# Seven pairs of hidden tiles start the MLP early instead of six, the last token tile's transposes stand nine steps behind its norm, and the last block's split comes first with its low part on GpSimd

## The chip, the cores and the metric

The kernel runs on one core of one Trainium2 chip. The engines are named as in the profile: PE (TensorE, matrix products; PEld its weight loads), DVE (VectorE), ACT (ScalarE), POOL (GpSimd), SP (SyncE, which here only issues DMAs). The metric is the device time of one execution in microseconds, and lower is better.

## What is computed

Two decoder layers over 1024 tokens of width 1024, in float32. Layer 0 mixes with a sparse attention of three branches, layer 1 with a sliding window; each is followed by a squared-ReLU MLP with 4096 hidden units. Cut to what the change touches:

```
for i in range(DEPTH):                       # DEPTH = 2
    ...
    y = mixer(modulate(rms_norm(x, norm_g[i, 0]), sh1, sc1))
    x = x + (1 + g1) * rms_norm(y, norm_g[i, 1])
    h = modulate(rms_norm(x, norm_g[i, 2]), sh2, sc2)
    a = relu(h @ mlp_w_up[i])                # 1024 x 1024 @ 1024 x 4096
    y = (a * a) @ mlp_w_down[i]
    x = x + (1 + g2) * rms_norm(y, norm_g[i, 3])
```

## The kernel before

**Products.** A float32 product is made of three matmuls of rounded parts (`mm3`, L572 to L574): each operand is split into a high part (`hh` of the tokens, by ACT at L1250; the first half of `wt` of the weights, by ACT at L1339) and a low part, value minus high part (`hl`, L1251, and the second half of `wt`, L1340, both DVE). A product of a 128-wide weight tile with 512 tokens over four k-tiles is 12 matmuls of 128x512.

**Seven products for eight.** `mlp_up` takes the hidden units as 16 pairs of 128-wide tiles, and the operands as 2x2 blocks. The tokens' blocks are B11 and B21 (token tiles 0 to 3, the two halves of the width) and B12 and B22 (token tiles 4 to 7). Of each pair it makes seven products with sums and differences of blocks. Products 1 (with B11) and 2 (with B21) need token tiles 0 to 3 alone; products 6, 5, 7, 3 and 4 need T1 = B12 - B11, B22 - T1, B22 - B12, B22 itself and B21 - (B22 - T1). Product 3 takes B22 as it is. Weights are summed for products 6 (L1322, L1323, DVE), 7 and 3 (L1329, L1333, POOL).

**The early products.** The MLP's products begin while the output projection of the attention is still finishing its last token tiles. `order` lists products 1 and 2 of the first `PAIRS0` pairs first (the early products, twelve for six pairs), then products 6, 5, 7, 3 and 4 of each of those pairs (the dependent products), then seven products for each later pair. An early pair's weights come as 512 KB for its products 1 and 2 (`load(q, True)`), and later again in two halves of 512 KB for the others (`load(q, False)`). `before(i)` says which weights are loaded and split ahead of the i-th product.

**The last token tile.** Token tiles arrive one by one. `done` queues for each: the stages of its norm (residual sum L522 on DVE, square on ACT, root on POOL L451, scaling into `xr` on DVE L472), then idle steps, then the steps of `tile(t)`: eight transposes on PE (`turn`, L1234), eight evacuations with the adaLN scale and shift on ACT (`put`, L1245), and `near` (L1266 on DVE for T1, L1267 on POOL for B22 - B12). For the last tile follow: `minus` on DVE (L1257, two of 128x1024: B22 - T1), the splits, and `minus` on POOL (L1257, two: B21 - (B22 - T1)). Each split is two pairs of instructions (two k-tiles each).

**Order and buffers.** The steps are handed out by `go`, `later` and `chain` between the products; from the program written so, a scheduler makes the row of instructions of each engine, and an engine takes its row strictly in order. The tiles of 4 KB per partition (`hr`, `hh`, `hl`, `wt`, `w`, `u`, `sx`) share 40 slots: an instruction or DMA that fills a tile waits until the slot's tile before it is done with. After its products a hidden pair's results (`u`) are combined on POOL (L1415, L1426) and written to DRAM by SP.

Of the kernel before, what the change touches and what calls it, by code (L numbers as in the profile page):

```python
# [9 lines left out]
F32 = mybir.dt.float32  # L10
# [4 lines left out]
ALU = mybir.AluOpType  # L15
# [7 lines left out]
NT = S // P  # L23
# [5 lines left out]
SLOTS = 40  # L29
UT = HID // P  # L30
LEAD_DOWN = 14
PAIRS0 = 6
TURN = (10, 20)
SIDE2 = 40
AHEAD = 3
DL = 4
# [57 lines left out]
class Trunk:  # L94
# [1126 lines left out]
    def up_setup(self, w_up, col):  # L1221
# [6 lines left out]
        nc = self.nc  # L1228
        R, raw, pts = {}, {}, {}

        def turn(t, xr, c):
            pts[t, c] = pt = self.bank()
            for k in range(4):
                nc.tensor.transpose(pt[:, k * P:(k + 1) * P], xr[t][:, (4 * c + k) * P:(4 * c + k + 1) * P], self.ident)  # L1234
            if c == 1:
                xr.pop(t)

        def put(t, c):
            pt, (A, B) = pts.pop((t, c)), col()
            for k in range(4):  # L1240
                n = (t // 4, c, k // 2)
                if t % 4 == 0 and k % 2 == 0:
                    raw[n] = self.slot("hr", F32, [P, 2, 512])
                f = 4 * c + k
                nc.scalar.activation(raw[n][:, k % 2, (t % 4) * P:(t % 4 + 1) * P], pt[:, k * P:(k + 1) * P], AF.Identity,  # L1245
                                     scale=A[:, f:f + 1], bias=B[:, f:f + 1])

        def split(p, r):
            hi, lo = (self.slot(x, F32R, [P, 2, 512]) for x in ("hh", "hl"))
            nc.scalar.activation(hi, r, AF.Copy)  # L1250
            nc.vector.tensor_tensor(lo, r, hi.bitcast(F32), op=ALU.subtract)  # L1251
            R.setdefault(p, []).append((hi, lo))

        def minus(eng, out, x, y):
            if out not in raw:
                raw[out] = self.slot("hr", F32, [P, 2, 512])
            eng.tensor_tensor(raw[out], raw[x], raw[y], op=ALU.subtract)  # L1257

        b11, b21, b12, b22, t1 = (lambda j, n=n: (*n, j) for n in ((0, 0), (0, 1), (1, 0), (1, 1), (2, 0)))

        def near(t, j):

            if t1(j) not in raw:
                raw[t1(j)] = self.slot("hr", F32, [P, 2, 512])
            v = lambda n: raw[n][:, :, (t - 4) * P:(t - 3) * P]
            nc.vector.tensor_tensor(v(t1(j)), v(b12(j)), v(b11(j)), op=ALU.subtract)  # L1266
            nc.gpsimd.tensor_tensor(v(b12(j)), v(b22(j)), v(b12(j)), op=ALU.subtract)  # L1267

        def tile(t, xr):
            steps = [lambda c=c: (turn(t, xr, c), put(t, c)) for c in range(2)]  # L1270
            if t > 3:
                steps.append(lambda: (near(t, 0), near(t, 1)))
            if t == 7:
                V, G = nc.vector, nc.gpsimd
                steps.append(lambda: [minus(V, b11(j), b22(j), t1(j)) for j in range(2)])
                for p, b in ((6, b11), (5, t1), (7, b12), (3, b22)):
                    if p == 5:
                        steps.append(lambda: [minus(G, b21(j), b21(j), b11(j)) for j in range(2)])
                    steps += [lambda p=p, b=b, j=j: split(p, raw[b(j)]) for j in range(2)]
                steps += [lambda j=j: split(4, raw[b21(j)]) for j in range(2)]  # L1280
            return steps


        n_q = UT // 2
        order = [(q + z, p) for q in range(0, PAIRS0, 2) for p in (1, 2) for z in range(min(2, PAIRS0 - q))]
        at = {}
        for q in range(n_q):
            at[q] = len(order)
            order += [(q, p) for p in ((6, 5, 7, 3, 4) if q < PAIRS0 else (1, 2, 6, 5, 7, 3, 4))]
        wraw, left, sums = {}, {}, {}  # L1290
        four = lambda v: v.rearrange("p (k c) -> p k c", k=4)

        def load(q, early):
            if early:
                r = self.raw_weight(self.raw if q < 3 else self.slot, w_up, list(range(KT)), 2 * q * P, P)
                r = r.rearrange("p (k c) -> p k c", k=KT)
                wraw[q] = {11: r[:, 0:4], 12: r[:, 4:8]}
            else:
                w = {}
                for c, alloc in ((0, self.raw), (1, self.slot)):  # L1300
                    r = self.raw_weight(alloc, w_up, list(range(4 * c, 4 * c + 4)), 2 * q * P, 2 * P)
                    r = r.rearrange("p (k c) -> p k c", k=4)
                    w[11 + c], w[21 + c] = r[:, :, 0:P], r[:, :, P:2 * P]
                wraw[q] = w

        def prep(i):

            q, p = order[i]
            w = wraw[q]
            early = i < at[0]  # L1310
            t = nc.vector.tensor_tensor

            def new(n):
                sums[n] = four(self.t2("ws"))
                return sums[n]

            if p == 1:
                r = w[11]
            elif p == 2:
                r = w[12]  # L1320
            elif p == 6:
                t(new(1), w[21], w[22], op=ALU.add)  # L1322
                t(new(2), sums[1], w[11], op=ALU.subtract)  # L1323
                r = sums[2]
            elif p == 5:
                r = sums.pop(1)
            elif p == 7:
                r = new(3)
                nc.gpsimd.tensor_tensor(r, w.pop(11), w.pop(21), op=ALU.subtract)  # L1329
                sums.pop(3)  # L1330
            elif p == 3:
                r = new(4)
                nc.gpsimd.tensor_tensor(r, w.pop(12), sums.pop(2), op=ALU.subtract)  # L1333
                sums.pop(4)
            else:
                r = w.pop(22)
            s = self.slot("wt", F32R, [P, 2, 512])
            hi, lo = (four(s[:, y]) for y in range(2))
            nc.scalar.activation(hi, r, AF.Copy)  # L1339
            nc.vector.tensor_tensor(lo, r, hi.bitcast(F32), op=ALU.subtract)  # L1340
            left[i] = s
            if early and p == 2 or p == 4:
                wraw.pop(q)
# [5 lines left out]
        def before(i):  # L1349

            out = [lambda n=n: prep(n) for n in range(len(order)) if when(n) == i]
            if i in (0, 1, 2):
                out += [lambda q=q: load(q, True) for q in (3 + i,) if q < PAIRS0]
            for q in range(n_q):
                if i == (2 if q == 0 else when(at[q] - 2)):
                    out.append(lambda q=q: load(q, False))
            return out
# [5 lines left out]
    def mlp_up(self, up, side, sd, begin):  # L1363
# [43 lines left out]
        def combine(q):  # L1407
            a, b = U.pop(q)
            d, z = sd[q], {}

            def two(n, *ops):
                def f():
                    z[n] = self.slot("sx", F32, [P, 2, 512])
                    for k, (x, y, op) in enumerate(ops):
                        nc.gpsimd.tensor_tensor(z[n][:, k], x, y, op=op)  # L1415
                return f

            def put():
                nc.sync.dma_start(d[:, 0], b[:, 1])
                nc.sync.dma_start(d[:, 5], a[:, 0])  # L1420
                nc.sync.dma_start(d[:, 1:3], z[0])

            def put2():
                nc.sync.dma_start(d[:, 3:5], z[1])
                v = self.t2("sy")
                nc.gpsimd.tensor_tensor(v, a[:, 1], b[:, 1], op=ALU.add)  # L1426
                nc.sync.dma_start(d[:, 6], v)

            A, B = ALU.add, ALU.subtract
            return [two(0, (a[:, 0], b[:, 1], A), (b[:, 0], b[:, 1], B)), put,  # L1430
                    two(1, (a[:, 0], b[:, 0], A), (a[:, 1], a[:, 0], B)), put2]

        ramp, steps = [], []
        for i, (q, p) in enumerate(order):
            own = spread(before(i), product(i))
            if p == 4:
                own.append(lambda q=q: self.later(lambda: self.chain(combine(q)), 1))
            (ramp if i < 2 * PAIRS0 + 10 else steps).extend(own)
        self.go(ramp)
# [204 lines left out]
    def run(self):  # L1644
        nc, a = self.nc, self.a
# [6 lines left out]
        xr = {}  # L1652
# [25 lines left out]
        loads, steps = parts[0]  # L1678
# [30 lines left out]
        for l in range(2):  # L1709
# [3 lines left out]
            xr = {}  # L1713
# [8 lines left out]
            take, up = self.up_setup(a["mlp_w_up"][l], lambda l=l: self.cols[l, 1])  # L1722

            def done(t, x, take=take, xr=xr, l=l):
                def turn():
                    self.chain([lambda: None] * (2 + DL if t == NT - 1 else TURN[l]) + take(t, xr))
                self.chain(self.norm_stages(x, xr, t) + [turn])

            if l == 0:
# [18 lines left out]
                for t in range(NT):  # L1748
                    steps = outs[t][1]
                    if t + 1 < NT:  # L1750
                        steps = [outs[t + 1][0]] + steps
                    else:
                        steps = spread(up[-1], steps)
# [85 lines left out]
```

## Time and profile before

| what | value |
|---|---|
| median of three runs | 2538.34 us (2536.49 to 2544.4) |
| the profiled execution | 2542.84 us, span 2541.1 us |
| mean granted clock of PE | 0.976 of full speed |
| PE busy | 2400.1 us, 94% of the span |
| DVE / ACT / POOL busy | 1921.1 / 1406.2 / 1321.5 us |
| share of the chain that ended last | PE 39%, DVE 5%, POOL 3%, ACT 2%, DMA 2% |

The span runs from the first to the last instruction of the profiled execution; its own time lies 1.7 us above it. The busy times are sums over the whole span. The early stretch of MLP-up, where the change sits, is about 900 to 1030 us in layer 0 and about 1890 to 2030 us in layer 1.

### The profile page before, as it was taken

What the parts mean: (1) busy time and instruction counts of PE and PEld (TensorE: products, weight loads), DVE (VectorE), ACT (ScalarE), POOL (GpSimd) and SP (SyncE); (2) the same over time, 40 slices, a digit from 0 to 9 for tenths busy, and PEclk for the clock granted to TensorE, in tenths of its full rate; (3) what the DMA queues carried; (4) which work ended last, traced back from release to release, by engine and by line L of the source; (5) the groups of instructions that cost most, each with busy time, mean ns of one, the idle gap of its engine ahead of it and who ended that gap; (6) DMA issues with size and microseconds to landing.
All of it is one profiled execution on the core that took longest, in us unless ns stands there. A gap on an engine that the chain in (4) does not pass through costs nothing.

```text
span 2541.1 us, 36695 instructions
## 1 busy us (share of the span) xinstructions
PE 2400.1 (94%) x11974; PEld 1993.6 (78%) x11974; DVE 1921.1 (76%) x3723; ACT 1406.2 (55%) x2959; POOL 1321.5 (52%) x1308
## 2 busy tenths in 40 slices
PE   6989999999998988999999999988999999999997
PEld 4779788888887766777788888877877788888886
DVE  6866479999996477778799868666767766687756
ACT  4632268888984473444435445467876354545433
POOL 4320466564662135555764622577744654694533
PEclk8999999999999999999999999999999999999999
DMA  7367723121226635555888755444324545597654
GB/s 279 100 218 237 236 88 94 41 88 43 85 70 154 141 116 181 200 195 199 294 325 335 238 182 185 142 137 121 75 77 132 181 170 185 192 318 240 229 184 172
DMA packets 239288, 437.15 MB, mean 172 GB/s; under 512 B 19236, under 2 KB 122872, under 8 KB 239096
## 3 DMA queue, kind: packets, MB, share of 16 engines
q1 hardware_dynamic: 210296, 405.44, 47.5%
q0 software_dynamic: 28800, 29.36, 4.8%
q8 instruction: 94, 1.54, 0.2%
q14 instruction: 98, 0.80, 0.1%
HBM read 320.42 MB, written 114.31 MB: 171 GB/s over the span
## 4 chain that ended last, share of the span: by engine, by line
PE 39%; DVE 5%; POOL 3%; issue 2%; ACT 2%; DMA 2%; SPq 0%; POOLq 0%; DVEq 0%; ACTq 0%
PE b L573 12%; PE b L572 12%; PE b L574 12%; POOL sx L1415 1%; PE b L880 1%; DMA wr<-in_mlp_w_down_dram 1%; DVE ada L323 1%; DMA adaw<-in_ada_w_dram 1%; ACT p L888 1%; DMA w<-in_mlp_w_up_dram 1%; DVE hl L1251 1%; DVE wt L1340 1%; POOL qv L637 1%; PE o L925 0%; DVE p L884 0%
## 5 line engine op out<-in xcount | busy, mean ns | idle before, releaser
L572 PE MATMUL b<-hh,wt 128*128 128x512 f32 x896 | 356.9, 398 | 15.7 <-ACT wt L1339 15.7
L574 PE MATMUL b<-hh,wt 128*128 128x512 f32 x896 | 352.3, 396 | 11.7 <-DVE wt L1340 11.5
L573 PE MATMUL b<-hl,wt 128*128 128x512 f32 x896 | 353.6, 395 | 0.0
L573 PE MATMUL b<-st,st 128*128 128x512 f32 x896 | 350.6, 392 | 2.7 <-DVE st L1489 2.7
L574 PE MATMUL b<-st,st 128*128 128x512 f32 x896 | 349.6, 391 | 0.0
L572 PE MATMUL b<-st,st 128*128 128x512 f32 x896 | 331.4, 391 | 2.7 <-DVE u L1370 1.6
L888 ACT ACTIVATE p<-p,nm 128x256 f32<-128x256 f32 (+7 forms) x384 | 251.1, 659 | 44.5 <-DVE nm L884 43.2
L1028 POOL TENSOR_SCALAR p<-p,rl,nsam 128x640 f32<-128x640 f32 (+7 forms) x256 | 200.5, 796 | 139.6 <-DVE rl L1026 96.1
L1489 DVE TENSOR_TENSOR st<-sr,st 128x1024 fp32r<-128x1024 f32 (+1 forms) x128 | 205.0, 1601 | 34.9 <-ACT st L1488 32.7
L910 DVE TENSOR_TENSOR pT<-b,pT 128x512 fp32r<-128x512 f32 (+1 forms) x334 | 215.1, 657 | 20.3 <-ACT pT L909 19.9
L1488 ACT ACTIVATE st<-wr 128x1024 fp32r<-128x1024 f32 (+1 forms) x128 | 122.7, 959 | 192.5 <-POOL wr L1474 85.0
L1489 DVE TENSOR_TENSOR st<-wr,st 128x1024 fp32r<-128x1024 f32 (+1 forms) x128 | 186.9, 1460 | 53.4 <-ACT st L1488 35.0
L572 PEld LDWEIGHTS b<-hh,wt 128*128 128x128 f32 x896 | 171.2, 191 | 57.9 <-ACT wt L1339 23.5
L574 PEld LDWEIGHTS b<-hh,wt 128*128 128x128 f32 x896 | 171.0, 191 | 55.0 <-DVE wt L1340 19.3
L909 ACT ACTIVATE pT<-b 128x512 fp32r<-128x512 f32 (+1 forms) x334 | 186.5, 580 | 42.2 <-PE b L903 41.0
L573 PEld LDWEIGHTS b<-st,st 128*128 128x128 f32 x896 | 169.0, 189 | 39.9 <-DVE st L1489 5.0
L572 PEld LDWEIGHTS b<-st,st 128*128 128x128 f32 x896 | 169.0, 189 | 39.3 <-DVE u L1370 2.4
L903 PE MATMUL b<-ident,p 128*128 128x128 f32 x1296 | 196.1, 275 | 3.9 <-DVE nm L884 1.8
L573 PEld LDWEIGHTS b<-hl,wt 128*128 128x128 f32 x896 | 171.4, 191 | 35.2
L1340 DVE TENSOR_TENSOR wt<-ws,wt 128x512 fp32r<-128x512 f32 x128 | 139.7, 1104 | 77.7 <-ACT wt L1339 77.0
L574 PEld LDWEIGHTS b<-st,st 128*128 128x128 f32 x896 | 168.9, 189 | 34.6
L925 PE MATMUL o<-pT,kv 128*128 128x512 f32 x484 | 193.0, 437 | 2.3 <-DVE pT L910 2.0
(277 smaller groups left out, 6042.4 us busy)
## 6 DMA issues: line engine op xcount, KB each, us to landing
adaw<-in_ada_w_dram SPq DMA_DIRECT2D x96, 512.0 KB, 4.8
sr<-s SPq DMA_DIRECT2D x96, 512.0 KB, 4.3
wr<-in_mlp_w_down_dram SPq DMA_DIRECT2D x96, 512.0 KB, 5.6
w<-in_mlp_w_up_dram SPq DMA_DIRECT2D x76, 512.0 KB, 4.9
s<-sx SPq DMA_DIRECT2D x64, 512.0 KB, 4.0
x<-x SPq DMA_DIRECT2D x48, 512.0 KB, 3.3
s<-u SPq DMA_DIRECT2D x64, 256.0 KB, 2.2
we<-in_mlp_w_down_dram SPq DMA_DIRECT2D x64, 256.0 KB, 4.4
```

Of the source, the lines that this page charges most:

```text
L572: mm(out, s[0], m[0], start=first, stop=False)
L573: mm(out, s[0], m[1], start=False, stop=False)
L574: mm(out, s[1], m[0], start=False, stop=last)
L888: self.nc.scalar.activation(p, p, AF.Exp, scale=-1.0, bias=nm, accum_out=l)
L903: nc.tensor.transpose(pt[:, g * P:(g + 1) * P], p[:, cols], self.ident)
L909: nc.scalar.activation(x[:, 0, 0:w], pt[:, 0:w], AF.Copy)
L910: nc.vector.tensor_tensor(x[:, 1, 0:w], pt[:, 0:w], x[:, 0, 0:w].bitcast(F32), op=ALU.subtract)
L925: nc.tensor.matmul(out, s, m[:, z], start=n == 0 and z == 0, stop=n == len(tiles) - 1 and z == 1)
L1028: nc.gpsimd.tensor_scalar(ps[g], ps[g], rl[:, g:g + 1], gate[:, g, b:b + 1], op0=ALU.mult, op1=ALU.mult)
L1340: nc.vector.tensor_tensor(lo, r, hi.bitcast(F32), op=ALU.subtract)
L1488: nc.scalar.activation(hi, r, AF.Copy)
L1489: nc.vector.tensor_tensor(lo, r, hi.bitcast(F32), op=ALU.subtract)
```

## The change

It is the same in both layers. Seven early pairs stand first (fourteen early products), so pair 6's early weights are loaded too (`before`). For the last token tile the split of B22 (product 3) is the first of the splits, and its two low parts are made by GpSimd; before they were on DVE behind the split for product 7. The last tile's steps stand nine idle steps behind its norm, instead of `2 + DL`, which is six. No work is added or left out but one more early load of 512 KB in each layer. Lines behind L1273 move by one (L1340 becomes L1341, L1370 L1371).

```diff
--- before.py
+++ after.py
@@ -29,7 +29,7 @@
 SLOTS = 40
 UT = HID // P
 LEAD_DOWN = 14
-PAIRS0 = 6
+PAIRS0 = 7
 TURN = (10, 20)
 SIDE2 = 40
 AHEAD = 3
@@ -1245,10 +1245,10 @@
                 nc.scalar.activation(raw[n][:, k % 2, (t % 4) * P:(t % 4 + 1) * P], pt[:, k * P:(k + 1) * P], AF.Identity,
                                      scale=A[:, f:f + 1], bias=B[:, f:f + 1])
 
-        def split(p, r):
+        def split(p, r, eng=None):
             hi, lo = (self.slot(x, F32R, [P, 2, 512]) for x in ("hh", "hl"))
             nc.scalar.activation(hi, r, AF.Copy)
-            nc.vector.tensor_tensor(lo, r, hi.bitcast(F32), op=ALU.subtract)
+            (eng or nc.vector).tensor_tensor(lo, r, hi.bitcast(F32), op=ALU.subtract)
             R.setdefault(p, []).append((hi, lo))
 
         def minus(eng, out, x, y):
@@ -1273,7 +1273,8 @@
             if t == 7:
                 V, G = nc.vector, nc.gpsimd
                 steps.append(lambda: [minus(V, b11(j), b22(j), t1(j)) for j in range(2)])
-                for p, b in ((6, b11), (5, t1), (7, b12), (3, b22)):
+                steps += [lambda j=j: split(3, raw[b22(j)], G) for j in range(2)]
+                for p, b in ((6, b11), (5, t1), (7, b12)):
                     if p == 5:
                         steps.append(lambda: [minus(G, b21(j), b21(j), b11(j)) for j in range(2)])
                     steps += [lambda p=p, b=b, j=j: split(p, raw[b(j)]) for j in range(2)]
@@ -1349,7 +1350,7 @@
         def before(i):
 
             out = [lambda n=n: prep(n) for n in range(len(order)) if when(n) == i]
-            if i in (0, 1, 2):
+            if i in (0, 1, 2, 3):
                 out += [lambda q=q: load(q, True) for q in (3 + i,) if q < PAIRS0]
             for q in range(n_q):
                 if i == (2 if q == 0 else when(at[q] - 2)):
@@ -1723,7 +1724,7 @@
 
             def done(t, x, take=take, xr=xr, l=l):
                 def turn():
-                    self.chain([lambda: None] * (2 + DL if t == NT - 1 else TURN[l]) + take(t, xr))
+                    self.chain([lambda: None] * (9 if t == NT - 1 else TURN[l]) + take(t, xr))
                 self.chain(self.norm_stages(x, xr, t) + [turn])
 
             if l == 0:
```

On PE, layer 0, at the end of the second early product (`b2400`), before; `xr2396` is the last token tile:

```order
L573 MATMUL b2400_10689<-hl2372_10537,wt2375_10550 128x512
L574 MATMUL b2400_10689<-hh2371_10536,wt2375_10550 128x512
L1234 MATMUL b2403_10708<-ident_67,xr2396_10674 128x128 x4
L1234 MATMUL b2405_10720<-ident_67,xr2396_10674 128x128 x4
L572 MATMUL b2406_10729<-hh2378_10577,wt2376_10559 128x512
L573 MATMUL b2406_10729<-hl2379_10578,wt2376_10559 128x512
```

and at the same place now, where the third early product (`b2404`, twelve rows) begins in the row that held the first transposes; its end:

```order
L572 MATMUL b2404_10711<-hh2385_10609,wt2376_10559 128x512
L573 MATMUL b2404_10711<-hl2386_10610,wt2376_10559 128x512
L574 MATMUL b2404_10711<-hh2385_10609,wt2376_10559 128x512
L1234 MATMUL b2406_10721<-ident_67,xr2396_10674 128x128 x4
L1234 MATMUL b2408_10732<-ident_67,xr2396_10674 128x128 x4
L572 MATMUL b2414_10767<-hh2378_10577,wt2388_10652 128x512
L573 MATMUL b2414_10767<-hl2379_10578,wt2388_10652 128x512
```

The third early product has moved ahead of the last tile's transposes; eleven early products follow them (ten before), and then product 6 of pair 0.

On DVE, layer 0, from the last tile's B22 - T1 (`minus`) on, before; `wt` are weights' low parts, `u` evacuations of products out of PSUM, `ws` weight sums:

```order
L1257 TENSOR_TENSOR hr2256_9985<-hr2347_10430,hr2349_10442 128x1024
L1257 TENSOR_TENSOR hr2257_9988<-hr2348_10433,hr2350_10445 128x1024
L1340 TENSOR_TENSOR wt2398_10685<-w2397_10683,wt2398_10685 128x512
L1340 TENSOR_TENSOR wt2401_10696<-w2364_10492,wt2401_10696 128x512
L1340 TENSOR_TENSOR wt2404_10717<-w2397_10683,wt2404_10717 128x512
L1370 TENSOR_TENSOR u2391_10659<-b2406_10729,u2391_10659 128x512
L1340 TENSOR_TENSOR wt2407_10740<-w2402_10706,wt2407_10740 128x512
L1251 TENSOR_TENSOR hl2410_10748<-hr2256_9985,hh2409_10747 128x1024
L1251 TENSOR_TENSOR hl2412_10761<-hr2257_9988,hh2411_10760 128x1024
L1370 TENSOR_TENSOR u2399_10688<-b2418_10777,u2399_10688 128x512
L1340 TENSOR_TENSOR wt2415_10770<-w2408_10745,wt2415_10770 128x512
```

and now:

```order
L1257 TENSOR_TENSOR hr2256_9985<-hr2347_10430,hr2349_10442 128x1024
L1257 TENSOR_TENSOR hr2257_9988<-hr2348_10433,hr2350_10445 128x1024
L1341 TENSOR_TENSOR wt2398_10685<-w2397_10683,wt2398_10685 128x512
L1341 TENSOR_TENSOR wt2401_10696<-w2364_10492,wt2401_10696 128x512
L1371 TENSOR_TENSOR u2399_10688<-b2414_10767,u2399_10688 128x512
L1341 TENSOR_TENSOR wt2403_10708<-w2397_10683,wt2403_10708 128x512
L1341 TENSOR_TENSOR wt2405_10718<-w2402_10706,wt2405_10718 128x512
L1341 TENSOR_TENSOR wt2411_10760<-w2407_10730,wt2411_10760 128x512
L1323 TENSOR_TENSOR ws2449_10943<-w2409_10754,w2410_10756 128x512
L1324 TENSOR_TENSOR ws2450_10945<-ws2449_10943,w2409_10754 128x512
L1341 TENSOR_TENSOR wt2417_10778<-w2402_10706,wt2417_10778 128x512
L1251 TENSOR_TENSOR hl2419_10782<-hr2256_9985,hh2418_10781 128x1024
```

More weights' low parts stand ahead of the first token low part (`hl`). From behind the second L1257 to the low part of the first dependent product's weights (`wt2445` before, `wt2451` now) the row held 8 `wt`, 4 `u`, 2 `ws` and 10 `hl`; now it holds 10 `wt`, 5 `u`, 2 `ws` and 8 `hl`. In layer 1 the same stretch held 5 `wt`, 2 `u`, 2 `ws` and 10 `hl`, and now holds 7 `wt`, 4 `u`, 2 `ws` and 8 `hl`.

On POOL, layer 0, from the last tile's B21 - (B22 - T1) on, before (L1329 and L1333 are weight sums of 128x512):

```order
L1257 TENSOR_TENSOR hr2259_10002<-hr2259_10002,hr2256_9985 128x1024
L1257 TENSOR_TENSOR hr2260_10005<-hr2260_10005,hr2257_9988 128x1024
L1329 TENSOR_TENSOR ws2450_10945<-w2413_10764 128x512
L1333 TENSOR_TENSOR ws2453_10966<-w2414_10766,ws2444_10906 128x512
L1329 TENSOR_TENSOR ws2467_11050<-w2457_10979 128x512
L1333 TENSOR_TENSOR ws2471_11074<-w2458_10981,ws2462_11009 128x512
```

and now:

```order
L1257 TENSOR_TENSOR hr2259_10002<-hr2259_10002,hr2256_9985 128x1024
L1257 TENSOR_TENSOR hr2260_10005<-hr2260_10005,hr2257_9988 128x1024
L1251 TENSOR_TENSOR hl2413_10764<-hr2347_10430,hh2412_10763 128x1024
L1330 TENSOR_TENSOR ws2456_10984<-w2409_10754 128x512
L1334 TENSOR_TENSOR ws2459_11005<-w2410_10756,ws2450_10945 128x512
L1251 TENSOR_TENSOR hl2416_10775<-hr2348_10433,hh2415_10774 128x1024
L1330 TENSOR_TENSOR ws2473_11089<-w2463_11018 128x512
L1334 TENSOR_TENSOR ws2477_11113<-w2464_11020,ws2468_11048 128x512
```

The two low parts of B22 (`hl`, 128x1024) stand around the first pair's weight sums. On SP the write of the first product's result (which waits for two ACT instructions that stand one ahead of and one behind the last tile's evacuations) now stands ahead of the loads of pair 5's early weights and of a second half of pair 0's.

## Rows read from the trace of the kernel before

**Rows 1.** The page's parts 1 (busy us, share, instructions) and 6 (KB each, us to landing).

```profile
PE 2400.1 (94%) x11974; PEld 1993.6 (78%) x11974; DVE 1921.1 (76%) x3723; ACT 1406.2 (55%) x2959; POOL 1321.5 (52%) x1308
...
w<-in_mlp_w_up_dram SPq DMA_DIRECT2D x76, 512.0 KB, 4.9
```

**Rows 2.** PE's waits, 890 to 1010 us: waiter <- releaser: us, times, longest.

```profile
PE b L1234 <- DVE xr L472: 6.1, 2, 4.8
PE b L574 <- DVE wt L1340: 5.7, 4, 2.9
PE b L572 <- ACT wt L1339: 5.7, 3, 2.3
```

**Rows 3.** PE's waits, 1860 to 2010 us (layer 1).

```profile
PE b L572 <- ACT wt L1339: 6.2, 5, 2.4
...
PE b L574 <- DVE wt L1340: 1.9, 3, 0.9
```

**Rows 4.** PE in time: start, us, line, out<-in [idle before].

```profile
905.64 0.39 PE L573 MATMUL b<-hl,wt 128*128 128x512 f32 x1
905.87 0.39 PE L574 MATMUL b<-hh,wt 128*128 128x512 f32 x1
911.10 1.97 PE L1234 MATMUL b<-ident,xr 128*128 128x128 f32 x8 [4.84 <-DVE xr L472]
...
913.29 0.63 PE L573 MATMUL b<-hl,wt 128*128 128x512 f32 x1
913.72 0.63 PE L574 MATMUL b<-hh,wt 128*128 128x512 f32 x1
```

**Rows 5.** PE in time: first dependent product's second matmul, layer 0, then 1.

```profile
944.34 0.50 PE L574 MATMUL b<-hh,wt 128*128 128x512 f32 x1 [2.06 <-DVE wt L1340]
...
1939.87 0.55 PE L574 MATMUL b<-hh,wt 128*128 128x512 f32 x1 [0.68 <-DVE wt L1340]
```

**Rows 6.** Busy us of each engine, granted clock, in both layers' early stretches.

```profile
911.00:945.00 34.00, 31.84 (x133) 26.20 (x134) 31.41 (x31) 24.66 (x41) 19.29 (x7) 0.92 0.43 130
1905.00:1945.00 40.00, 35.24 (x147) 27.82 (x148) 37.02 (x39) 30.29 (x53) 16.55 (x9) 0.96 0.41 126
```

**Rows 7.** DVE in time, layer 0.

```profile
914.49 2.90 DVE L1257 TENSOR_TENSOR hr<-hr,hr 128x1024 f32<-128x1024 f32 x2 [0.27 <-ACT hr L1245]
917.31 6.85 DVE L1340 TENSOR_TENSOR wt<-w,wt 128x512 fp32r<-128x512 f32 x3
...
925.81 2.35 DVE L1251 TENSOR_TENSOR hl<-hr,hh 128x1024 fp32r<-128x1024 f32 x2
...
928.68 0.68 DVE L1340 TENSOR_TENSOR wt<-w,wt 128x512 fp32r<-128x512 f32 x1
...
943.61 1.88 DVE L1340 TENSOR_TENSOR wt<-ws,wt 128x512 fp32r<-128x512 f32 x3
```

**Rows 8.** POOL in time, layer 0.

```profile
917.95 5.66 POOL L1257 TENSOR_TENSOR hr<-hr,hr 128x1024 f32<-128x1024 f32 x2
...
933.52 6.22 POOL L1333 TENSOR_TENSOR ws<-w,ws 128x512 f32<-128x512 f32 x1 [8.17 <-DVE ws L1323]
```

**Rows 9.** DVE in time, layer 1, then POOL.

```profile
1914.06 1.21 DVE L1257 TENSOR_TENSOR hr<-hr,hr 128x1024 f32<-128x1024 f32 x1
1915.19 2.89 DVE L1340 TENSOR_TENSOR wt<-w,wt 128x512 fp32r<-128x512 f32 x1
...
1939.14 0.68 DVE L1340 TENSOR_TENSOR wt<-ws,wt 128x512 fp32r<-128x512 f32 x1
...
1914.10 6.25 POOL L1257 TENSOR_TENSOR hr<-hr,hr 128x1024 f32<-128x1024 f32 x2
```

**Rows 10.** PE in time, layer 0: stalls behind later pairs' weights.

```profile
975.09 0.50 PE L572 MATMUL b<-hh,wt 128*128 128x512 f32 x1 [2.35 <-ACT wt L1339]
...
1023.12 0.50 PE L572 MATMUL b<-hh,wt 128*128 128x512 f32 x1 [0.74 <-ACT wt L1339]
...
1025.79 0.80 PE L572 MATMUL b<-hh,wt 128*128 128x512 f32 x1 [1.41 <-ACT wt L1339]
```

## The prediction

> **What bounds the kernel now.** I read the page first: PE is busy for 94% of the span [rows 1], so a change that leaves the products as they are can only win back PE's idle time or its slow clock, and the question is which of that lies where the change works. The list of PE's waits over the two early stretches of MLP-up answers it. In layer 0, from 890 to 1010 us, PE waits 6.1 us for the scaled last token tiles (4.8 of it at once), 5.7 us for weights' low parts on DVE and 5.7 us for weights' high parts on ACT [rows 2]; in layer 1 6.2 us for ACT and 1.9 us for DVE [rows 3]. The list in order of time puts places to them: PE ends its second early product at about 906.3, stands for 4.84 us until the last tile's transposes at 911.10, and runs the next matmuls 0.43 us apart where they were 0.23 apart before (913.29 to 913.72 against 905.64 to 905.87) [rows 4]; that is half speed, the lower of its two clock levels, after an idle time. At 944.34 it waits another 2.06 us for the low part of the first dependent product's weights [rows 5]. Over 911 to 945 the granted clock is 0.92 and DVE is busy 31.41 of 34 us; over 1905 to 1945 in layer 1 it is 37.02 of 40 [rows 6]. So the reader should see two limits in one place: PE has holes, and DVE, which makes every low part, has almost none. The first hole comes from the last tile's norm, the second from DVE's row.
>
> **The change, part by part.** The two added early products of each layer are moved, not added: what they are worth is PE time that is spent before the first dependent product rather than behind it. Twelve matmuls at 0.23 us are 2.7 us, two products 5.4 us. The gain of a layer is therefore 5.4 us less the time by which the first dependent product starts later than it does now (944.3 and 1939.8 [rows 5]), as long as what follows keeps its distances.
>
> *The nine steps.* The third early product now stands ahead of the last tile's transposes. It can start when the second ends, at 906.3, and is done by 909.0, inside the 4.84 us hole [rows 4]: the transposes wait for xr at 911.10 as before. Its evacuation on DVE (0.68 us, as its other 128x512 instructions [rows 7]) and a relu on ACT come ahead of the last tile's work on those engines; both end before 911, so their cover is the same hole. If the product came 2 us late they would push the chain by what is over.
>
> *PE's way to the first dependent product.* Eleven early products follow the transposes instead of ten. If these take 1.1 us at full speed (they took 1.97 at half [rows 4]), PE would be there at 912.2 + 11 x 2.7, about 942, were nothing late. So PE is not what sets that product's start: the low part of its weights is, on DVE.
>
> *DVE's row, layer 0.* The stretch runs from the end of the last minus (914.49 + 2.90 = 917.4) to the end of the first dependent low part (943.61 + 0.68 = 944.3) [rows 7], 26.9 us. Undisturbed instructions of 128x512 follow one another every 0.60 us (three in 1.88), those of 128x1024 every 1.14 (two in 2.35, the last of them 1.21) [rows 7]. The row held 14 small and 10 large ones: 8.4 + 11.4 = 19.8 us. The other 7.1 us are no idle time of DVE: they are instructions that took longer. Three low parts of weights took 6.85 us in place of 1.88 [rows 7] while POOL ran its two large subtractions, 5.66 us [rows 8]; in layer 1 one took 2.89 in place of 0.68 beside the same pair, 6.25 us [rows 9]. So one large subtraction on POOL costs DVE, by that row, 2.2 us. Now the row holds 17 small and 8 large ones: 10.2 + 9.1 = 19.3 us. DVE's own work falls by only 0.5 us, since three more small instructions for pair 6 come ahead of the first dependent low part as two large ones leave.
>
> *B22's low parts on POOL.* No POOL instruction of this line is in the trace; the nearest is the large subtraction with the same shape and two operands from the same memory, 2.83 us beside DVE [rows 8]. What each costs DVE lies between nothing (the one time that POOL took 6.22 us for a small subtraction, it was POOL that waited, and not DVE [rows 8]) and 2.83 us. I take 2.2, since DVE's row is as dense as where 2.2 was seen: 4.4 us a layer. The stretch becomes 19.3 + 7.1 + 4.4 = 30.8 us and ends at 948.2. The page "SBUF — State Buffer" of the Trainium skill (section "Who interferes with whom") speaks against this edit: a DVE instruction with two inputs in SBUF and a GpSimd one that reads SBUF exclude each other, and the second to issue is fully blocked. The 2.89 us in place of 0.68 agree [rows 9].
>
> Layer 0 then gains 5.4 - (948.2 - 944.3) = 1.5 us.
>
> *Layer 1.* From 1914.06 + 1.21 = 1915.3 to 1939.14 + 0.68 = 1939.8 [rows 9] are 24.5 us: 9 small and 10 large instructions, 16.8 us, and 7.7 us of waits for POOL. Now 13 small and 8 large ones: 16.9 + 7.7 + 4.4 = 29.0, end at 1944.3. Gain 5.4 - 4.5 = 0.9 us.
>
> *The loads.* Pair 5's early weights and a second half of pair 0's now wait on SP behind a write whose data ACT finishes behind the last tile's evacuations, near 916. With 4.9 us to landing [rows 1] they are there near 921 to 922; DVE comes to them behind two or three low parts, of which each was slow (to 924.2 [rows 7]). I cost it at nothing; the cover is about 2 us, and a landing later than that is paid in full, because everything in DVE's row stands behind it. Pair 6's added 512 KB lie behind that. The slot it holds is missing for the second halves of pairs 1 to 5: see the last rival.
>
> *Sum.* 1.5 + 0.9 = 2.4 us. Against the profiled execution, 2542.84, that is 2540.4; it lies 4.5 us above the median of 2538.34, whose runs spread over 7.9 us, so I forecast from the median: 2536 us. A measurement of this kernel can tell about 0.3%, 7.6 us, from no change. Two corrections are left out of the sum and kept in the range: POOL may slip in where DVE reads PSUM and cost less (up to 4.4 us a layer), and the new hole on PE may cost clock.
>
> **The rivals.**
>
> *A. POOL waits, not DVE.* If B22's low parts find the pair of operands free, or stand aside as the one 6.22 us instruction did [rows 8], no wait is added. The stretches end at 943.8 and 1939.9, the gains are 5.9 and 5.3 us, and the time is 2527.1: faster by 0.44%. For it speaks that row; against it the three instructions that took 6.85 us. The same page of the Trainium skill has it that the order of issue decides who is blocked; by that, DVE's back-to-back rows would come first and this would be the time, and the 6.22 us are such a case.
>
> *B. The hole moves and takes the clock along.* PE reaches the first dependent product near 942 and waits until 948: 6 us, more than the 4.84 that was followed by half speed, where the present 2.06 at the same place is not in the way. A granted clock of 0.92 over 34 us is 2.7 us lost [rows 6]. Lost behind the hole in both layers, it turns 2.4 us of gain into 3.0 of loss: 2541.3, within the bound. It needs PE to be the limit behind the hole; DVE's next low parts come every 0.60 us, so it is for a few products.
>
> *C. Slots.* This one ends slower. With seven early weight tiles and fourteen early products, the second halves of pairs 1 to 5 are loaded later than now in relation to the products that need them. By the row of SP's instructions pair 5's is let go behind one product more, 2.7 us, and pair 3's behind a write of pair 0's result, about 1 us by my estimate. Their products stall already: 2.35 us at 975.09 for pair 2, 0.74 and 1.41 at 1023 to 1026 for pair 5 [rows 10], so there is no cover. 3.7 us a layer less the gain make 2538.34 + 7.4 - 2.4 = 2543.3. It decides (over 2546) from 5 us a layer on, that is if one more pair's load comes a whole product late: three loads late by 2.7 us in each layer are 16.2 us, and 2552. Against it: where the dependent products shift, their loads and their needs shift together.
>
> **How the numbers follow.** My forecast has a chance of 0.47, A 0.21, B 0.20, C 0.12 (0.07 of it over the bound). The likeliest case gives 2536, its own range, from half of 2.2 us to the full 2.83 for each low part on POOL, being 2531.5 to 2538.5. The range of 2526.5 to 2544 takes in A, B and the lower part of C. Faster by over 0.3% (under 2530.7) is most of A, 0.18; slower is C's upper part, 0.07; the rest, 0.75, is within.
>
> **What would show it.** In the profile after: (1) no idle time of 4.8 us ahead of the last tile's transposes, a product there at 0.23 us a matmul, and no half speed behind it. (2) Low parts of 128x512 on DVE of over 2 us beside POOL's L1251; if these stay at 0.68, A holds. (3) The first dependent product at about 948 and 1944 if the starts of the layers are unmoved, with PE waiting for L1341 ahead of it by some 6 us; a start by 944 is A. (4) Waits for L1340 and L1341 between 960 and 1030 that grow by 3 us or more are C. The forecast is wrong above all if DVE's 7.1 us of waits are not a sum of POOL's instructions, so that two more don't add to them, or if the loads behind SP's write land late.

## The result and the profile after

The changed kernel takes 2551.75 us (2550.2 to 2555.85, 5 runs) against 2538.34 (2536.49 to 2544.4, 5 runs): a ratio of 1.0054, interval 1.0042 to 1.0066. It is 13.4 us slower, by more than the 0.3% that can be told, and outside the forecast's range. Its profiled execution took 2550.2 us.

The busy times have hardly moved, as for a change that only moves work (the page's part 1; before in [rows 1]):

```profile
PE 2399.8 (94%) x11974; PEld 1993.4 (78%) x11974; DVE 1934.2 (76%) x3719; ACT 1400.7 (55%) x2959; POOL 1334.9 (52%) x1312
```

PE's waits, first from 890 to 1010 us, then from 1860 to 2010, answer to [rows 2] and [rows 3]:

```profile
PE b L574 <- DVE wt L1341: 8.8, 6, 3.0
PE b L572 <- ACT wt L1340: 4.3, 3, 2.1
PE b L1234 <- DVE xr L472: 2.9, 2, 1.6
```

```profile
PE b L574 <- DVE wt L1341: 9.9, 5, 4.0
PE b L572 <- ACT wt L1340: 3.0, 2, 2.3
```

The long wait for the last tile's scaled tokens is gone (2.9 us in place of 6.1). Waits for weights' low parts have taken its place: 8.8 us against 5.7 in layer 0, and 9.9 against 1.9 in layer 1. Those for high parts on ACT became shorter (4.3 against 5.7, and 3.0 against 6.2), so that the three together fall from 17.5 to 16.0 us in layer 0, while the two of layer 1 grow from 8.1 to 12.9. PE in order of time shows where, in layer 0 (before in [rows 4] and [rows 5]):

```profile
908.39 0.39 PE L573 MATMUL b<-hl,wt 128*128 128x512 f32 x1
908.62 0.39 PE L574 MATMUL b<-hh,wt 128*128 128x512 f32 x1
910.63 1.10 PE L1234 MATMUL b<-ident,xr 128*128 128x128 f32 x8 [1.62 <-DVE xr L472]
911.48 0.48 PE L572 MATMUL b<-hh,wt 128*128 128x512 f32 x1
911.80 0.39 PE L573 MATMUL b<-hl,wt 128*128 128x512 f32 x1
912.03 0.40 PE L574 MATMUL b<-hh,wt 128*128 128x512 f32 x1
912.27 0.39 PE L572 MATMUL b<-hh,wt 128*128 128x512 f32 x1
...
937.44 0.80 PE L574 MATMUL b<-hh,wt 128*128 128x512 f32 x1 [3.04 <-DVE wt L1341]
...
948.45 0.50 PE L574 MATMUL b<-hh,wt 128*128 128x512 f32 x1 [0.58 <-DVE wt L1341]
```

The third early product runs up to the transposes at 0.23 us a matmul, these wait 1.62 us, and there is no half speed behind them (from 911.80 on a matmul starts every 0.23 to 0.24 us): the nine steps did what was forecast. Then 3.04 us are lost inside the early products, and the first dependent product's low part lets PE go on at 948.45 (944.34 before), where the forecast had 948.2.

DVE beside POOL, layer 0; first DVE, then POOL, each in order of time (before in [rows 7] and [rows 8]):

```profile
913.96 2.91 DVE L1257 TENSOR_TENSOR hr<-hr,hr 128x1024 f32<-128x1024 f32 x2 [0.27 <-ACT hr L1245]
916.79 4.03 DVE L1341 TENSOR_TENSOR wt<-w,wt 128x512 fp32r<-128x512 f32 x2
...
921.35 5.72 DVE L1341 TENSOR_TENSOR wt<-w,wt 128x512 fp32r<-128x512 f32 x3
926.99 1.80 DVE L1323 TENSOR_TENSOR ws<-w,w 128x512 f32<-128x512 f32 x1
...
930.03 5.65 DVE L1251 TENSOR_TENSOR hl<-hr,hh 128x1024 fp32r<-128x1024 f32 x2
...
947.72 1.28 DVE L1341 TENSOR_TENSOR wt<-ws,wt 128x512 fp32r<-128x512 f32 x2
```

```profile
923.63 2.88 POOL L1251 TENSOR_TENSOR hl<-hr,hh 128x1024 fp32r<-128x1024 f32 x1 [0.55 <-ACT hh L1250]
...
931.23 3.38 POOL L1251 TENSOR_TENSOR hl<-hr,hh 128x1024 fp32r<-128x1024 f32 x1
```

The stretch from the end of L1257 (913.96 + 2.91) to the end of the first dependent low part (947.72 + 0.68) is 31.5 us, where 30.8 were forecast. Each of B22's low parts on POOL took 2.9 to 3.4 us, and DVE's instructions beside them lengthened: two low parts in 5.65 us against 2.35 undisturbed [rows 7].

**A ledger of the two early stretches.** To see where the time went I took from each trace the 128x512 matmuls of MLP-up, twelve to a product, and cut the stretch from the end of the 24th (two products) to the end of the 588th (forty-nine; both kernels have then done the same work) into three: the rest of the early products, pair 0's five dependent ones, and all that follows. From each I took 2.72 us for each of its products; what is left is lost time. It is worked out from the matmuls' rows and stands for all runs in one table (us; "free" is the number of slots less 28 for the split tokens, seven products' four tiles each, and less one `u` for each early pair):

| kernel | ratio to before | free | layer 0: early, pair 0, after | layer 1: early, pair 0, after | sum |
|---|---|---|---|---|---|
| before | 1 | 6 | 8.4, 3.1, 16.0 | 3.9, 5.9, 9.9 | 47.1 |
| **the change** | 1.0054 | 5 | 8.0, 2.4, 17.7 | 8.7, 2.6, 18.6 | 58.0 |
| seven pairs alone | 1.0012 | 5 | 8.4, 1.4, 14.7 | 6.0, 3.9, 15.5 | 49.8 |
| nine steps alone | 0.9996 | 6 | 3.7, 8.6, 10.0 | 1.8, 8.9, 9.8 | 42.7 |
| B22 on POOL alone | 1.0014 | 6 | 8.7, 6.1, 15.4 | 8.6, 2.2, 9.8 | 50.7 |
| nine steps, B22 on POOL | 1.0012 | 6 | 8.0, 7.0, 9.7 | 3.8, 10.1, 10.2 | 48.9 |
| seven pairs, nine steps | 1.0041 | 5 | 5.1, 3.6, 18.0 | 3.6, 4.7, 21.1 | 56.0 |
| seven pairs, B22 on POOL | 1.0064 | 5 | 10.4, 5.4, 14.8 | 8.6, 1.9, 19.5 | 60.6 |
| the change, B22 on DVE | 1.0034 | 5 | 5.2, 3.3, 18.3 | 5.7, 4.3, 19.2 | 56.0 |
| before, five pairs | 1.0008 | 7 | 8.4, 7.4, 14.1 | 2.8, 12.1, 6.8 | 51.6 |
| before, 39 slots | 1.0123 | 5 | 8.4, 4.0, 17.6 | 3.9, 6.7, 16.9 | 57.5 |
| before, 41 slots | 0.9954 | 7 | 8.6, 5.1, 9.7 | 3.7, 6.6, 8.0 | 41.7 |
| the change, 41 slots | 0.9984 | 6 | 8.6, 0.9, 13.9 | 7.1, 1.2, 14.0 | 45.7 |
| nine steps, 41 slots | 0.9939 | 7 | 4.0, 7.8, 9.0 | 1.8, 9.6, 7.5 | 39.7 |

The sums of the two first rows differ by 10.8 us, the medians by 13.4: most of the loss lies in these two stretches. The two profiled spans differ by 7.2 us only, so outside the stretches the one after is 3.6 us shorter, which is less than the 7.9 us over which before's five executions spread. Up to the end of pair 0's dependent products the change loses 21.7 us and before 21.3, so the forecast's gain of 2.4 us there is missing too; 10.4 of the 10.8 us come behind, 1.7 in layer 0 and 8.7 in layer 1. Each part is one execution's. With six pairs and 40 slots layer 1's last part is 9.8 to 10.2 in all four kernels; layer 0's is 16.0 and 15.4 with six steps, and 10.0 and 9.7 with nine.

### The profile page after: what moved, and what is told of

It reads as the page before. It is cut to its first block, busy times and chain, and to the rows that moved or that the text cites. A ratio compares the mean times of both kernels' runs of the same rounds, so it can differ in the third digit from the quotient of the medians.

```text
span 2548.3 us, 36705 instructions
## 1 busy us (share of the span) xinstructions
PE 2399.8 (94%) x11974; PEld 1993.4 (78%) x11974; DVE 1934.2 (76%) x3719; ACT 1400.7 (55%) x2959; POOL 1334.9 (52%) x1312
## 4 chain that ended last, share of the span: by engine, by line
PE 61%; DVE 14%; DMA 8%; issue 6%; POOL 5%; ACT 4%; SPq 1%; POOLq 0%; DVEq 0%; ACTq 0%
PE b L573 15%; PE b L574 15%; PE b L572 15%; PE b L880 5%; PE o L925 4%; PE b L903 4%; DMA w<-in_mlp_w_up_dram 2%; DVE p L884 2%; DVE wt L1341 1%; DVE ada L323 1%; DMA w<-in_nsa_w_in_dram 1%; DMA adaw<-in_ada_w_dram 1%; DMA o<-o 1%; DVE pT L910 1%; PE b L1033 1%
## 5 line engine op out<-in xcount | busy, mean ns | idle before, releaser
L910 DVE TENSOR_TENSOR pT<-b,pT 128x512 fp32r<-128x512 f32 (+1 forms) x334 | 214.8, 657 | 18.3 <-ACT pT L909 17.9
L1341 DVE TENSOR_TENSOR wt<-ws,wt 128x512 fp32r<-128x512 f32 x128 | 144.4, 1141 | 78.0 <-ACT wt L1340 76.7
```

The source lines that it names most:

```text
L910: nc.vector.tensor_tensor(x[:, 1, 0:w], pt[:, 0:w], x[:, 0, 0:w].bitcast(F32), op=ALU.subtract)
```

## The experiments

Theory 1: the forecast's rival C. The seventh pair's `u` takes one of the few slots that are free, so the second halves of the weights come late, pair by pair. Theory 2: B22's low parts on POOL take DVE's time, as the forecast costed them. Theory 3: the nine steps push the chain. The expectations say where a theory is meant more narrowly. The ratios are of 4 to 12 runs beside before on the same chip.

**One part at a time.** Seven pairs alone:

```diff
-PAIRS0 = 6
+PAIRS0 = 7
-            if i in (0, 1, 2):
+            if i in (0, 1, 2, 3):
```

> Seven early pairs alone, the nine steps and the split of B22 as before. Theory 1 (the seventh pair holds a slot from its early products to its late combination and takes an early load, so the second-half weight loads of the early pairs come later and every pair's product 6 waits for its summed weights): slower by 10 to 17 us, most of the change's 13.4 us, with PE's waits for L1340 and ACT's L1339 lines between 965 and 1050 us at least as long as in the changed kernel. Theory 2 (B22's low parts on POOL take DVE's time): within 4 us of before or faster, since the early products fill PE's hole and POOL has nothing more to do.

Measured: 1.0012 (1.0003 to 1.0021), 3 us slower. That is far less than theory 1 said, and inside theory 2's 4 us; but layer 1 loses 15.5 us in its last part against 9.9.

Nine steps alone:

```diff
-self.chain([lambda: None] * (2 + DL if t == NT - 1 else TURN[l]) + take(t, xr))
+self.chain([lambda: None] * (9 if t == NT - 1 else TURN[l]) + take(t, xr))
```

> The nine steps alone, six early pairs. Both theories: the third early product moves ahead of the last tile's transposes, the hole of 4.8 us shrinks to about 1.6, and a hole of 2 to 5 us opens ahead of the first dependent product because DVE's row is no shorter: between 3 us faster and no change. If the steps were the cause (theory 3: the last tile's chain is pushed), slower by over 6 us.

Measured: 0.9996 (0.9987 to 1.0005), no difference. The early products lose 3.7 and 1.8 us in place of 8.4 and 3.9, and most of that comes back ahead of the first dependent product (8.6 and 8.9 in place of 3.1 and 5.9), as expected. Theory 3 falls.

B22's split first, its low parts on POOL, alone:

```diff
-                for p, b in ((6, b11), (5, t1), (7, b12), (3, b22)):
+                steps += [lambda j=j: split(3, raw[b22(j)], G) for j in range(2)]
+                for p, b in ((6, b11), (5, t1), (7, b12)):
```

> B22's split first with its low parts on POOL, six early pairs and six steps. Theory 1: within 4 us of before, no slot is taken for longer. Theory 2: slower by 6 to 14 us, with the first dependent product's low part on DVE later by 3 us or more in each layer and long waits for L1340 behind it.

Measured: 1.0014 (1.0005 to 1.0022), 3.6 us slower: inside theory 1's 4 us, and less than theory 2 said. The trace shows the price of POOL's low parts all the same. Layer 1, first DVE, then POOL:

```profile
1913.65 2.90 DVE L1341 TENSOR_TENSOR wt<-w,wt 128x512 fp32r<-128x512 f32 x1
1916.48 2.90 DVE L1323 TENSOR_TENSOR ws<-w,w 128x512 f32<-128x512 f32 x1
1919.30 2.90 DVE L1341 TENSOR_TENSOR wt<-w,wt 128x512 fp32r<-128x512 f32 x1
1922.12 2.88 DVE L1324 TENSOR_TENSOR ws<-ws,w 128x512 f32<-128x512 f32 x1
```

```profile
1912.56 3.43 POOL L1257 TENSOR_TENSOR hr<-hr,hr 128x1024 f32<-128x1024 f32 x1
1915.96 2.86 POOL L1251 TENSOR_TENSOR hl<-hr,hh 128x1024 fp32r<-128x1024 f32 x1
1918.79 2.86 POOL L1257 TENSOR_TENSOR hr<-hr,hr 128x1024 f32<-128x1024 f32 x1
1921.60 2.84 POOL L1251 TENSOR_TENSOR hl<-hr,hh 128x1024 fp32r<-128x1024 f32 x1
```

Four small instructions of DVE in a row take 2.9 us each in place of 0.68 [rows 7], beside two low parts and two subtractions on POOL. With that, 4.7 us more are lost among the early products of layer 1 (8.6 for 3.9); 3.7 of them come back in pair 0's part (2.2 for 5.9). In layer 0 the early products lose 0.3 us more (8.7 for 8.4), and pair 0's part 3.0 (6.1 for 3.1).

The last two together, with six pairs (both diffs above):

> The changed kernel with six early pairs in place of seven: nine steps and B22 on POOL. Theory 1: the loss is gone, between 5 us faster than before and 2 us slower. Theory 2: slower by 8 us or more, as the change.

Measured: 1.0012 (1.0003 to 1.002). That is between the theories, 1 us over theory 1's bound. The loss falls from 13.4 to 3 us when the seventh pair is taken back, so most of it needs the seventh pair; alone that one costs 3 us too.

**Pairs of parts, and the slot itself.** Seven pairs and nine steps:

> Seven pairs and nine steps, B22 split as before (last but one, on DVE). Theory 1 (the seventh pair takes one of the few slots that are free in the ramp, and the loads of the second halves come late): this holds the slot as the change does, so most of the loss: 7 to 13 us slower. Theory 2 (the loss needs B22's low parts on POOL beside the seventh pair, since both add to what precedes the first dependent product): 0 to 4 us slower, like seven pairs alone.

Measured: 1.0041 (1.0029 to 1.0052), 10.4 us slower, without B22's low parts on POOL. Theory 2 in its narrow form falls.

Seven pairs and B22 on POOL:

> Seven pairs and B22 first with its low parts on POOL, six steps as before. Theory 1: 7 to 13 us slower. Theory 2: 8 to 14 us slower, the whole of the change's loss. Together with the run without POOL's low parts: if both are near the sum of their parts (about 2 and 6 us), the three parts of the change interact only when all are there.

Measured: 1.0064 (1.005 to 1.0077), 16 us slower, more than either theory said, with more lost among the early products of both layers together than in any other run (10.4 and 8.6) and layer 1's last part at 19.5.

One slot more, in the kernel before and in the changed one; the squares' unused output goes into the tile that is written next, and `imps` and `impt` lose their second buffer, to make room:

```diff
-SLOTS = 40
+SLOTS = 41
-        junk = self.small([P, 1024], BF16, name="junk", bufs=1)
...
-            u["ss"] = self.sumsq(x)
+            out[t] = self.slot(name="xr")
+            u["ss"] = self.sumsq(x, out[t])
...
-            nc.scalar.activation(junk[:, 0:512], y(h), AF.Square, accum_out=u["ss"][:, h:h + 1])
+            nc.scalar.activation(u["t"][:, sl(h)], y(h), AF.Square, accum_out=u["ss"][:, h:h + 1])
...
-        s = self.small([P, 65], name="imps", bufs=2)
+        s = self.small([P, 65], name="imps", bufs=1)
```

> Control: the kernel before with 41 slots in place of 40; room for it is made by writing the unused output of the squares into the tile that is written next, and two small tiles lose their second buffer. Theory 1: the ramp's stalls behind products 6 of pairs 2 to 5 shorten, 2 to 6 us faster, most of it between 960 and 1050 us and between 1970 and 2040. Theory 2: within 2 us of before.

> The changed kernel with 41 slots, room made in the same way. Theory 1: the lost slot is given back, so 8 us or more of the 13.4 are gone: between 5 us faster than before and 5 us slower. Theory 2: the slot changes little, still 9 us or more slower than before.

Measured: before with 41 slots 0.9954 (0.9941 to 0.9967), 12 us faster; the change with 41 slots 0.9984 (0.9975 to 0.9993), 4 us faster than before, 17.5 us better than with 40. In the two stretches this gives the change 12.3 us (58.0 to 45.7), and before 5.4, inside what theory 1 had said; the rest lies in other stages, which were not taken apart. The slot and the edits that make room for it came together: with 40 slots those edits were not run alone. Beside before with 41 slots the change with 41 is still 7.9 us slower (2531.41 against 2523.56 us).

One slot less, in the kernel before (`SLOTS = 39`, nothing else):

> The kernel before with 39 slots and nothing else changed. Theory 1 (slots set the ramp's pace): the two early stretches of MLP-up, from the end of the second product to the end of the forty-ninth, become longer by 4 to 12 us together, as with the seventh pair alone, and the whole is slower by 8 to 20 us, since other stages use the slots too. Theory 2 (the seventh pair costs by its instructions ahead of the first dependent product, not by its slot): the stretches stay within 2 us.

Measured: 1.0123 (1.0109 to 1.0137), 31 us slower, more than the 8 to 20 expected; 10.4 of it, as expected, lie in the two stretches, with six pairs, six steps and POOL as before. Layer 1's last part is 16.9, near that of seven pairs alone (15.5). Where DVE waits in layer 1, 1940 to 2062 us, in this kernel, in the changed one, in before, in before with 41 slots and in the change with 41:

```profile
DVE ws L1322 <- DMA w<-in_mlp_w_up_dram: 12.4, 5, 5.3
...
DVE u L1370 <- DMA s<-sx: 3.4, 1, 3.4
```

```profile
DVE ws L1323 <- DMA w<-in_mlp_w_up_dram: 14.3, 6, 3.4
...
DVE u L1371 <- DMA s<-sx: 4.3, 1, 4.3
```

```profile
DVE ws L1322 <- DMA w<-in_mlp_w_up_dram: 4.5, 3, 1.8
```

```profile
DVE ws L1320 <- DMA w<-in_mlp_w_up_dram: 6.1, 4, 2.0
```

```profile
DVE ws L1321 <- DMA w<-in_mlp_w_up_dram: 8.5, 5, 3.2
```

With five free slots, by either way, DVE waits 12 to 14 us for the weights' second halves in this view (all six kernels of the table), and 3.4 to 7.6 for a slot for an evacuation (`u`) that a write of combined results (`sx`) still holds; with six or seven it is 4.4 to 6.1 us (8.5 in the change with 41), and there is no such slot wait. This is the main evidence for theory 1, and it is layer 1's. In layer 0, 945 to 1060 us, the wait for the second halves doesn't show it: 11.0 us before, 3.0 after.

B22 first, but its low parts on DVE, all else as in the change (`split(3, raw[b22(j)])` without `G`):

> The changed kernel with B22's low parts back on DVE, still the first split. If POOL's low parts block DVE, as the prediction costed it (4.4 us a layer), this is 3 to 9 us faster than the changed kernel: 4 to 10 us slower than before. If only the place of the split matters, it is within 3 us of the changed kernel, 10 to 16 us slower than before.

Measured: 1.0034 (1.0022 to 1.0045), 8.6 us slower than before, about 5 us better than the change. The early products lose 5.2 and 5.7 us in place of 8.0 and 8.7.

Five early pairs (`PAIRS0 = 5` in the kernel before):

> The kernel before with five early pairs. Theory 1: one slot more is free in the ramp, the stalls ahead of later pairs' product 6 shrink by 2 to 8 us, but PE has two products less to fill its time before the first dependent product, about 5 us a layer: between 3 us faster and 8 us slower. Theory 2: 6 to 11 us slower, the early products' time twice.

Measured: 1.0008 (0.9999 to 1.0018). Pair 0's part grows (7.4 and 12.1 us in place of 3.1 and 5.9: PE has fewer products to fill its time), and the last part shrinks (14.1 and 6.8 in place of 16.0 and 9.9). It loses on one side what it gains on the other.

Nine steps with 41 slots:

> 41 slots and the nine steps, six pairs, B22 as before: what the runs point to as the best. 11 to 16 us faster than before. With 40 slots the nine steps alone were 1 us faster; if freed slots let their filled hole count, it is 2 to 4 us faster than 41 slots alone.

Measured: 0.9939 (0.9924 to 0.9954), 15.5 us faster than before, the fastest version: 2520.43 us. PE's waits, 880 to 1010 us, where the transposes (L1232 here) cost 2.4 us, about as in the changed kernel, and the longest wait is now for high parts on ACT:

```profile
PE b L570 <- ACT wt L1337: 9.3, 3, 4.9
...
PE b L1232 <- DVE xr L471: 2.4, 2, 1.9
```

## Why the prediction was wrong, point by point

The sum's own terms held, but for the place where PE waits. *Nine steps*: the hole of 4.84 us became 1.62, without a slow clock behind it. *DVE's row*: 31.5 us against 30.8 forecast in layer 0; the first dependent product went on 4.1 us later against 3.9. In layer 1 the stretch is 29.6 us (1913.13 to 1942.69) against 29.0. *POOL's price*: 31.5 less DVE's own 19.3 less the 7.1 that were there before leaves 5.1 us for two low parts, 2.5 each against 2.2; the run with these on DVE gives about 5 us back over both layers, where the sum gives 4.2 (8.8, less four instructions of 1.14 us that DVE then makes itself). Rival A, by which POOL would wait and not DVE, is out. *Where PE waits* was wrong in the place: not 6 us ahead of the first dependent product but 3.04 us inside the early ones, whose weights' low parts stand behind the same blocked row; in layer 1 it is 3.96 us. DVE's stretch and PE's hole in layer 1, and the busy times and granted clock of both stretches (before in [rows 6]):

```profile
1910.23 2.90 DVE L1257 TENSOR_TENSOR hr<-hr,hr 128x1024 f32<-128x1024 f32 x2 [0.19 <-ACT hr L1245]
...
1942.01 1.28 DVE L1341 TENSOR_TENSOR wt<-ws,wt 128x512 fp32r<-128x512 f32 x2
...
1931.73 0.79 PE L574 MATMUL b<-hh,wt 128*128 128x512 f32 x1 [3.96 <-DVE wt L1341]
...
911.00:945.00 34.00, 30.96 (x132) 24.64 (x131) 32.03 (x26) 22.57 (x38) 20.93 (x9) 0.95 0.46 135
1905.00:1945.00 40.00, 36.04 (x149) 29.07 (x148) 36.86 (x31) 28.37 (x48) 21.06 (x10) 0.91 0.34 105
```

In layer 1 the clock is 0.91 where it was 0.96, so a part of rival B came true: 0.05 of 40 us, 2 us. That is about what layer 1 misses against the forecast (1.5 us lost up to pair 0's end, for 0.9 gained); layer 0, at 0.95 for 0.92, gains 1.1 of its 1.5.

*The step that failed* is the condition under the gain, "as long as what follows keeps its distances", and with it the size and the chance of rival C. What follows lost 10.4 us, 1.7 in layer 0 and 8.7 in layer 1, where C had 3.7 in each, asked 5 of each to pass the bound, and had a chance of 0.12; I held against it that loads and needs shift together. In layer 1 they did not: a load waits for a slot that earlier results hold. C's upper case, three loads late by 2.7 us in each layer, came to 2552 us, beside the 2551.75 measured; that is luck, since the layers lose 1.7 and 8.7 and not 8.1 each. Its sign, waits between 960 and 1030 us that grow by 3 us or more, did not come (9.1 us before, 10.3 after); they grow in layer 1, from 5.2 to 11.5 us between 1958 and 2059, and behind pair 0 the granted clock there is 0.95 where it was 0.98. C also read the stalls at 1023 to 1026 us [rows 10] as pair 5's; they lie in pair 4's products (1010.6 to 1028.7). After, layer 1, SP, then DVE, then PE:

```profile
1982.10 0.32 SPq L1422 DMA_DIRECT2D s<-sx  x1
1985.07 0.38 SPq L547 DMA_DIRECT2D w<-in_mlp_w_up_dram  x1
```

```profile
1989.56 0.69 DVE L1323 TENSOR_TENSOR ws<-w,w 128x512 f32<-128x512 f32 x1 [2.27 <-DMA w<-in_mlp_w_up_dram]
```

```profile
1989.51 0.39 PE L574 MATMUL b<-hh,wt 128*128 128x512 f32 x1
1992.23 0.80 PE L572 MATMUL b<-hh,wt 128*128 128x512 f32 x1 [2.33 <-ACT wt L1340]
```

Pair 1's last product ended near 1974.8; its combined results are handed to a write at 1982.10; the load of pair 3's second half gets its slot at 1985.07, lands 4.5 us later, DVE makes the sum at 1989.56, and PE, whose row has product 6 of pair 3 next, starts it at 1992.23. What SP waits for ahead of that load, after (1984 to 1985.2 us), and ahead of the same load before (1973.8 to 1975.1):

```profile
SPq L547 <- DMA s<-sx: 2.3, 1, 2.3
```

```profile
SPq L547 <- POOL sx L1415: 1.2, 1, 1.2
```

Before, the load of pair 3 waits until POOL has combined pair 1's results; now until they are written. Such waits of a load for a write of combined results (940 to 1062 us, 1940 to 2060) number none in the three kernels with seven free slots, one in each layer in the five with six, and two in each with five; in layer 1 seven pairs alone, and seven pairs with B22 on POOL, have one. So the results of a pair hold up the weights of the pair two behind it, which is a loop; it is shown for these loads. Ahead of the loads of pairs 4 and 5 SP waits longest for DVE's `ada` instructions (L321, L323; the adaLN's weights, side work): 2.5 and 5.4 us after, 5.5 and 4.3 before.

In layer 1, pairs 3, 4 and 5, the load comes 10.3, 11.8 and 12.0 us after the last product of the pair two ahead; 10.0, 11.6 and 12.0 in before with 39 slots; 6.9, 10.7 and 10.4 before; 4.4, 10.5 and 10.1 in before with 41. Two pairs are 27.2 us of products; where the way from last product to load (10 to 12 us), from load to product 6 (7 to 10) and through the pair's own five products (13.6) is longer than that, each pair stalls. A slot less lengthens the first piece, for pair 3 most, and the lost time adds up over the pairs. That the early products which were gained only bring PE to these stalls sooner is argued, not shown.

What stays open: seven pairs alone cost 3 us, with the nine steps 10.4, though the nine steps by themselves cost nothing. By the ledger the nine steps shorten layer 0's last part with six pairs (16.0 to 10.0, and 15.4 to 9.7 with B22 on POOL), and with seven they lengthen it (14.7 to 18.0, 14.8 to 17.7); layer 1's, hardly moved with six, goes from 15.5 to 21.1 with seven, though with B22 on POOL from 19.5 to 18.6. Which slot goes to whom in which order was not separated. That the 7.9 us which the change costs with 41 slots are again its one slot (six free for seven) was not tested. With 41 slots the change still loses 14.0 us in layer 1's last part, where before with as many free slots loses 9.9; that it sends one pair more through the loop without early products between is argued, not shown.

## What to carry to other kernels

Before moving work forward, count what it holds while it waits: here 28 of 40 buffers were pinned and each early pair pinned one more, so one pair took one of six, and the lost time appeared up to 100 us behind the place that was improved. A stall that ends with a load is read back to what gave the load its buffer; if that is the result of an earlier round, the stage is a loop, and filling holes ahead of it may gain nothing. A change of the number of buffers by one, in both directions, tests this at once.

## What the runs showed that was not expected

One slot of 4 KB per partition is worth 31 us of 2538 when taken away from the kernel before, and 12 when added (with the edits that make room for it); nothing in the page's busy times hints at it. POOL and DVE alternated where both had a row of instructions with two operands in SBUF (layer 1 of the run with B22 on POOL alone): DVE's 128x512 instruction of 0.68 us took 2.9 us each time, four times in a row, while POOL's 128x1024 ones, behind the first, took 2.84 to 2.86 us. The page "SBUF — State Buffer" of the Trainium skill (section "Who interferes with whom") says that the two exclude each other; these rows agree. Its other rule, that the order of issue decides who is blocked, stood beside rival A; here the two took turns, and DVE was not spared.
